# A transformer block pair in fp32 on one core: the feature-by-token products take one 512-column matmul for two of 256

## The chip, the cores and the metric

The kernel runs on one core of a Trainium2 chip. TensorE (PE) multiplies; a 128x128 tile of one operand is loaded into it (LDWEIGHTS, PEld in the profile) and the other operand moves through it, up to 512 columns at a time, into a bank of PSUM of 128 partitions by 512 fp32 numbers. VectorE (DVE), ScalarE (ACT) and GpSimd (POOL) work element by element, and SyncE (SP) issues most of the DMAs. Each engine takes its instructions in the order in which they stand in its own queue, and waits for the others by semaphores. The metric is the time of one execution in microseconds of device time, the median of the runs.

## The reference

Two blocks follow each other on 256 tokens of 1024 features, all in fp32. Cut to what matters here:

```python
def first_block(x, ...):
    h = rms_norm(x, pre_mix_norm[l])
    proj = jnp.einsum('bsd,dc->bsc', h, w_in[l])
    att_q, att_k, att_v, gdn_qkv, gdn_z, gdn_a, gdn_b = jnp.split(proj, split_points, axis=-1)
    o_att = moba_attention(att_q, att_k, att_v, rel_bias)        # 8 heads of 64
    o_gdn = gated_deltanet(gdn_qkv, gdn_z, gdn_a, gdn_b, ...)    # conv of width 4, chunks of 64
    mix = jnp.einsum('bsc,cd->bsd', jnp.concatenate([o_att, o_gdn], axis=-1), w_out[l])
    x = x + rms_norm(mix, post_mix_norm[l])
    h = rms_norm(x, pre_mlp_norm[l])
    m = einsum(square(relu(einsum(h, w_up[l]))), w_down[l])      # 1024 -> 4096 -> 1024
    return x + rms_norm(m, post_mlp_norm[l])

def second_block(x, ...):
    proj = rmsnorm(x, g_mix[l]) @ w_in[l]    # xc, gb, gc, q, k, v, g_sw, gate_a, gate_r
    y_a = (gb * conv(gc * xc)) @ w_a_out[l]
    y_r = (group_norm(retention(rotary(q), rotary(k), v)) * silu(g_sw)) @ w_r_out[l]
    x = x + (sigmoid(gate_a) * y_a + sigmoid(gate_r) * y_r) @ w_o[l]
    h2 = rmsnorm(x, g_ffn[l])
    x = x + (silu(h2 @ w_ff_gate[l]) * (h2 @ w_ff_up[l])) @ w_ff_down[l]   # width 2816
    return rmsnorm(x, g_final)
```

## The kernel before

**Products.** Every large product is made of three: an operand is split into a rounded part H (a copy to the type float32r, on ACT) and a remainder L (the operand less its rounded part, on DVE), and the product is H·H + H·L + L·H, added up in one bank. `load_w` (L208) brings 512 KB of weights by a DMA on SP's queue into one of three buffers (`raw`), and splits them into `wh` on ACT (a line shown as L144, the helper `act`) and `wl` on DVE (L147, the helper `tt`), of which there are six buffers each.

**Two shapes.** Token-by-feature products (`gemm_tok_steps`, `GemmK`, `gemm_head`) move 512 columns of weights past a loaded tile of the activations. Feature-by-token products (`gemm_ch_steps`, L271) move the 256 tokens of the activations past a loaded tile of weights: for 128 features there are eight steps over the 1024 features of the input, of three matmuls of 256 columns each (H·XH, H·XL, L·XH at L222 and L281), 24 in all. Two such rounds (f = 0, 1) fill the two halves of one bank, and `evac` reads the whole bank. These products make q, k, v of the delta rule (`qkv`, six products) and q, k of the attention (`att_in`, four), 12 products of `w_up`, the eight rotary ones (`rot_evac`), 12 of the convolution branch of block two, and 18 of `w_ff_gate` and `w_ff_up`: 60 products, 120 rounds, 960 steps of three matmuls.

**Operands.** The activations `X` are a `Chan`: tiles `xTh` and `xTl` of [128, 2, 256]. `row_T` turns a normalised row on PE and `split_T` writes both parts.

**Buffers.** `SLOTS` says how many tiles each tag of the pool in SBUF holds, `BANKS` how the eight banks of PSUM are shared: three for these products (`mm`), three for the delta rule and the transposes (`sd`), two for the attention (`at`).

**Order.** A scheduler sets each engine's order when the program is built. In the first mixer the products are steps of a generator, and `go` puts some of them between the parts of the delta rule. Its longest serial piece: the products of keys in a chunk (`m`, DVE), written to DRAM (`md`) and read back one block to a partition (`mb`), fifteen steps of substitution on POOL (`tb`, `tmpb`, `ub`), to DRAM again (`ud`) and back (`U`), which PE then needs.

Of the kernel before, what the change touches and what calls it, by code (L numbers as in the profile page):

```python
# [41 lines left out]
SLOTS = {"t": 20, "g": 26, "j": 2, "n": 4, "h": 5, "k": 8}  # L42
# [55 lines left out]
def body(ctx: ExitStack, tc: tile.TileContext, I: dict, cst: bass.AP, out: bass.AP, dbg=None):  # L98
# [70 lines left out]
    @contextmanager  # L169
    def after(what):  # L170
        """what is traced here is issued behind the last instruction of that kind"""
        if what in last:
            with tc.issue_after(last[what].ins):
                yield
        else:
            yield
# [52 lines left out]
    class Chan:  # L229
        """[feature, token] operand: pairs of 128-feature tiles, rounded part and remainder"""  # L230
# [12 lines left out]

    def gemm_tok_steps(w, c0, X, evac):
        """[token, 512 features], a step for every two rows of 128 of the weights"""
# [14 lines left out]
    def put_off(f, n):  # L260
        """f is traced n pieces of a product later"""
        later.append([n, f])
# [7 lines left out]

    def gemm_ch_steps(w, c0, X, evac):  # L271
        """[256 features, token], a step for every 128 features"""
        ps = mmps()
        for f in range(2):
            H, L = load_w(w, 0, 8, c0 + f * P, P)
            o = ps[:, f * 256:(f + 1) * 256]
            for k in range(8):
                XH, XL = X.at(k)
                mm(o, H[:, k, :], XH, k == 0, False)
                mm(o, H[:, k, :], XL, False, False)  # L280
                last["step"] = nc.tensor.matmul(o, L[:, k, :], XH, start=False, stop=k == 7)  # L281
            if f == 1:
                evac(ps)
# [13 lines left out]
    class GemmK:  # L297
        """[token, D], 128 rows of the weights at a time; at the end token tile by token tile"""
# [33 lines left out]
        def finish(self, X, tail=((0, TAIL), (1, TAIL))):  # L332
            """tail: (token tile, number of rows of 128)"""
# [12 lines left out]
    def gemm_head(groups, X):  # L346
        """two groups of [token, 512 features], six of their eight loads first for one token tile"""
# [25 lines left out]
    def split_T(ps, X, k0, t, scale=None):  # L373
        """four transposed 128-feature tiles in a bank to operands"""
# [13 lines left out]
    def rms_of(srcs, gate="xs"):  # L388
        """1 / sqrt(mean of squares + eps) over the two halves of a row"""
# [42 lines left out]
    X = Chan(8, "xT")  # L432
# [4 lines left out]
    # per-channel vectors, turned into columns  # L437
# [14 lines left out]
    # head scalars on every partition  # L452
# [12 lines left out]
    def log1p_exp_neg_abs(src, n):  # L465
        """log(1 + exp(-|src|))"""
# [11 lines left out]
    # ================= block 1: mixer =================  # L478
# [8 lines left out]
    def hb(ap):  # L487
        """[P, 8] for every one of 64 columns"""
        return ap[:, :, None].to_broadcast([P, 8, 64])

    def cb(name):
        """[P, 64] for every head"""
        return C(name)[:, None, :].to_broadcast([P, 8, 64])

    def pe(ap, e):
        """heads of parity e of a [P, 8 * 64] tile"""
        return ap.rearrange("p (a e d) -> p a e d", a=4, e=2)[:, :, e, :]

    # ---- products with w_in and attention over the one block of keys: the work that fills the
    # gaps of the delta rule; each step yields its size ----  # L500
# [5 lines left out]
    def qkv(i):  # L506
        """q, k, v of the delta rule: convolution and SiLU, [channel, token]"""
# [16 lines left out]
    def att_in(i):  # L524
        def qk_evac(ps):
            s_ = T2("aqk")
            act(s_, ps, AF.Copy)
            (QT if i < 2 else KT)[i % 2] = s_.rearrange("p (a n) -> p a n", a=2)

        yield from gemm_ch_steps(w_in, 256 * i, X, qk_evac)  # L530
# [15 lines left out]
    # relative-position bias: [q, head, key], masked where the key is ahead  # L546
# [13 lines left out]
    def bias_tile(a, e):  # L560
        """heads of parity e, pair a"""
# [6 lines left out]
    def logits(a, e):  # L568
        """heads of parity e, pairs (2a, 2a+1 of that parity)"""
# [89 lines left out]
    def go(what):  # L659
        """fill for a time, or until a mark"""  # L660
# [17 lines left out]
    # a, b  # L678
# [40 lines left out]
    # decays between the rows of a chunk, and from its start and to its end  # L719
# [30 lines left out]
    def inv_norm(p_, name):  # L750
        """1 / sqrt(sum of squares + eps) of every head's 64 columns"""
# [593 lines left out]
```

## Time and profile before

| | |
|---|---|
| three runs | 938.85, 939.85, 940.24 us; median 939.85 us |
| the profiled execution, from its first to its last instruction | 935.1 us |
| median less that span | 4.75 us |
| PE busy with matmuls | 907.8 us (97%), 6069 matmuls |
| DVE busy | 564.5 us (60%) |
| ACT busy | 455.5 us (49%) |
| POOL busy | 93.4 us (10%) |
| read from HBM | 158.59 MB, 173 GB/s over the span |

The trace has the span of the profiled execution and not what lies around it, so its own time on the scale of the runs is taken as the span and the 4.75 us that the median has beyond it. Busy times are unions: an engine that works on two instructions at once counts once. A matmul's duration in the trace is longer than the distance to the next one, since matmuls follow each other through the array; what a matmul costs in a dense stretch is the distance of its start to the next start.

### The profile page before, as it was taken

To read this page: it belongs to the slowest core of one execution; us is meant where nothing else is said; L and a number is where in the kernel's file an instruction comes from. 1 tells how busy PE (TensorE), PEld (TensorE's weight loads), DVE (VectorE), ACT (ScalarE), POOL (GpSimd) and SP (SyncE) were. 2 spreads that over 40 slices of the span, in tenths; PEclk is the share of its full clock that TensorE was granted. 3 is DMA by queue.
4 is the path that set the end of the run, shared out by engine and by line. 5 is a ranking of instruction groups with operands and counts; after the bars stand their busy time and mean duration, and the time that the engine had idled before them with its cause. 6 is when DMAs were issued, how large, how long until landed. Compare 5 with 4: busy or idle time off the path is not lost.

```text
span 935.1 us, 15099 instructions
## 1 busy us (share of the span) xinstructions
PE 907.8 (97%) x6069; PEld 805.7 (86%) x6069; DVE 564.5 (60%) x771; ACT 455.5 (49%) x641; POOL 93.4 (10%) x127
## 2 busy tenths in 40 slices
PE   5999899999999999999999999999999999999997
PEld 5798787778998888799988899988888789999886
DVE  4897445376766544877656666645456755555443
ACT  4875263356656443655455554345343545444432
POOL 4168001020000000203200000000000000000000
PEclk9999899999999999999999999999999999999999
DMA  9775532156765765576534556566474567666551
GB/s 280 195 192 147 142 119 91 46 180 183 222 182 169 241 192 176 174 225 205 183 122 151 155 170 186 176 194 199 159 225 149 168 190 204 189 182 182 184 177 45
DMA packets 177142, 162.48 MB, mean 174 GB/s; under 512 B 18941, under 2 KB 144169, under 8 KB 177073
## 3 DMA queue, kind: packets, MB, share of 16 engines
q1 hardware_dynamic: 175200, 156.49, 56.1%
q0 software_dynamic: 1728, 4.78, 1.6%
q8 instruction: 47, 0.77, 0.3%
q10 hardware_dynamic: 144, 0.26, 0.1%
q14 instruction: 23, 0.18, 0.1%
HBM read 158.59 MB, written 2.92 MB: 173 GB/s over the span
## 4 chain that ended last, share of the span: by engine, by line
PE 83%; DMA 5%; DVE 4%; ACT 3%; issue 2%; POOL 2%; SPq 0%; POOLq 0%; ACTq 0%; DVEq 0%
PE mm L222 58%; PE mm L281 10%; PE at L222 7%; PE sd L222 6%; DVE wl L147 1%; DMA raw<-in_w_in_dram 1%; DVE acc L150 1%; POOL tb L147 1%; ACT wh L144 1%; POOL tmpb L147 1%; DMA hs<-in_dec_b_dram 1%; DMA raw<-in_w_up_dram 1%; DMA U<-ud 1%; ACT junk L392 1%; DMA mb<-md 1%
## 5 line engine op out<-in xcount | busy, mean ns | idle before, releaser
L147 DVE TENSOR_TENSOR wl<-raw,wh 128x1024 fp32r<-128x1024 f32 (+1 forms) x287 | 350.1, 1225 | 261.9 <-ACT wh L144 259.2
L144 ACT ACTIVATE wh<-raw 128x1024 fp32r<-128x1024 f32 (+1 forms) x287 | 302.3, 1057 | 354.4 <-PE mm L222 133.5
L222 PE MATMUL mm<-xTh,wh 128*128 128x256 f32 x960 | 273.3, 285 | 1.0 <-ACT wh L144 1.0
L281 PE MATMUL mm<-xTh,wl 128*128 128x256 f32 x960 | 271.9, 283 | 1.8 <-DVE wl L147 1.8
L222 PE MATMUL mm<-xTl,wh 128*128 128x256 f32 x960 | 271.9, 283 | 0.0
L281 PEld LDWEIGHTS mm<-xTh,wl 128*128 128x128 f32 x960 | 184.2, 192 | 2.2 <-DVE wl L147 2.2
L222 PEld LDWEIGHTS mm<-xTh,wh 128*128 128x128 f32 x960 | 184.1, 192 | 2.1 <-ACT wh L144 1.4
L222 PEld LDWEIGHTS mm<-xTl,wh 128*128 128x128 f32 x960 | 184.2, 192 | 0.1
L222 PE MATMUL mm<-wh,xTh 128*128 128x512 f32 x264 | 104.6, 396 | 1.2 <-ACT xTh L381 1.2
L222 PE MATMUL mm<-wh,xTl 128*128 128x512 f32 x264 | 103.7, 393 | 1.5 <-DVE xTl L384 1.5
L222 PE MATMUL mm<-wl,xTh 128*128 128x512 f32 x264 | 103.6, 392 | 0.0
L222 PE MATMUL mm<-wh,hidh 128*128 128x512 f32 x162 | 63.3, 391 | 0.1
L222 PE MATMUL mm<-wl,hidh 128*128 128x512 f32 x162 | 63.3, 391 | 0.0
L222 PE MATMUL mm<-wh,hidl 128*128 128x512 f32 x162 | 63.0, 389 | 0.0
L222 PEld LDWEIGHTS mm<-wh,xTl 128*128 128x128 f32 x264 | 49.7, 188 | 13.0 <-DVE xTl L384 2.8
L222 PEld LDWEIGHTS mm<-wh,xTh 128*128 128x128 f32 x264 | 49.7, 188 | 12.8 <-ACT xTh L381 1.9
L222 PEld LDWEIGHTS mm<-wl,xTh 128*128 128x128 f32 x264 | 49.7, 188 | 10.0 <-DVE wl L147 0.2
L396 POOL TENSOR_TENSOR r<-ms,neghalf 128x1 f32<-128x1 f32 x13 | 10.7, 827 | 466.9 <-DVE ms L150 466.9
L222 PEld LDWEIGHTS mm<-wh,hidl 128*128 128x128 f32 x162 | 30.4, 188 | 6.5
L222 PEld LDWEIGHTS mm<-wh,hidh 128*128 128x128 f32 x162 | 30.5, 188 | 6.3 <-issue 0.5
L222 PEld LDWEIGHTS mm<-wl,hidh 128*128 128x128 f32 x162 | 30.5, 188 | 5.5
L392 ACT ACTIVATE junk<-x 128x512 f32<-128x512 f32 x18 | 11.3, 627 | 17.9 <-DVE x L147 12.9
(359 smaller groups left out, 1146.3 us busy)
## 6 DMA issues: line engine op xcount, KB each, us to landing
raw<-in_w_in_dram SPq DMA_DIRECT2D x116, 512.0 KB, 4.3
raw<-in_w_up_dram SPq DMA_DIRECT2D x32, 512.0 KB, 4.1
raw<-in_w_down_dram SPq DMA_DIRECT2D x32, 512.0 KB, 4.2
raw<-in_w_ff_gate_dram SPq DMA_DIRECT2D x22, 512.0 KB, 4.1
raw<-in_w_ff_up_dram SPq DMA_DIRECT2D x22, 512.0 KB, 4.5
raw<-in_w_ff_down_dram SPq DMA_DIRECT2D x22, 512.0 KB, 4.0
raw<-in_w_r_out_dram SPq DMA_DIRECT2D x16, 512.0 KB, 3.9
raw<-in_w_out_dram SPq DMA_DIRECT2D x8, 512.0 KB, 3.5
```

The lines of the kernel that those rows point to most:

```text
L144: nc.scalar.activation(o, i, f, **kw)
L147: (eng or nc.vector).tensor_tensor(o, a, b, op=op)
L150: nc.vector.scalar_tensor_tensor(o, a, s, b, op0=op0, op1=op1)
L222: nc.tensor.matmul(o, a, b, start=start, stop=stop)
L281: last["step"] = nc.tensor.matmul(o, L[:, k, :], XH, start=False, stop=k == 7)
L392: last["sq"] = nc.scalar.activation(T2("junk", tag="j"), srcs[i], AF.Square, scale=1.0 / 32, accum_out=ss[:, i:i + 1])
L396: last["pow"] = nc.gpsimd.tensor_tensor(r, ms, neghalf[:, :1], op=ALU.pow)
```

## The change

`X` becomes a `Both` in all four places: one tile [128, 2, 2, 256] for a pair of feature tiles, in which a feature tile's 256 rounded columns and its 256 remainder columns lie side by side. A step of a feature-by-token product is then two matmuls: H against both parts, 512 columns wide, which leaves H·XH in the left half of a bank and H·XL in the right half, and L·XH, 256 columns, on top of the left half. A round of 128 features so takes a bank of its own. When it is read, ACT copies the right half to SBUF and DVE adds the left half to it; two rounds make a [128, 512] tile `sum`, and `evac` reads that tile in place of the bank. For `att_in` and for `xc` in the convolution branch the `sum` tile is the result itself, and their copies of the bank are gone. The tags of the pool are shared out anew.

```diff
-SLOTS = {"t": 20, "g": 26, "j": 2, "n": 4, "h": 5, "k": 8}
+SLOTS = {"t": 12, "x4": 4, "s2": 2, "g": 24, "j": 2, "n": 4, "h": 5, "k": 8}
...
+    class Both:
+        def __init__(self, name):
+            self.b = [T2(name, F32R, [P, 2, 2, S], "x4") for _ in range(4)]
+            self.h = [b[:, :, 0, :] for b in self.b]
+            self.l = [b[:, :, 1, :] for b in self.b]
+        at = Chan.at
+        def both(self, k):
+            return self.b[k // 2][:, k % 2, :, :]
...
-    def gemm_ch_steps(w, c0, X, evac):
-        ps = mmps()
+    def gemm_ch_steps(w, c0, X, evac, into=None):
+        s_ = into or T2("sum", tag="s2")
         for f in range(2):
             H, L = load_w(w, 0, 8, c0 + f * P, P)
-            o = ps[:, f * 256:(f + 1) * 256]
+            ps = mmps()
             for k in range(8):
-                XH, XL = X.at(k)
-                mm(o, H[:, k, :], XH, k == 0, False)
-                mm(o, H[:, k, :], XL, False, False)
-                last["step"] = nc.tensor.matmul(o, L[:, k, :], XH, start=False, stop=k == 7)
+                mm(ps, H[:, k, :], X.both(k), k == 0, False)
+                last["step"] = nc.tensor.matmul(ps[:, :S], L[:, k, :], X.at(k)[0], start=False, stop=k == 7)
+            half = s_[:, f * S:(f + 1) * S]
+            act(half, ps[:, S:], AF.Copy)
+            tt(half, ps[:, :S], half, ADD)
             if f == 1:
-                evac(ps)
+                evac(s_)
...
-    X = Chan(8, "xT")
+    X = Both("xT")
...
-        gemm_ch(w2, 256 * i, X, lambda ps: act(xc, ps, AF.Copy))
+        gemm_ch(w2, 256 * i, X, lambda ps: None, xc)
```

What the change does to the order, at three places. On PE, the first product of `w_up` that is made feature by token (`mm` is the bank, `xT` the activations, `wh` and `wl` the split weights); before, two steps of its first round:

```order
L222 MATMUL mm_2479<-xTh_2163,wh_2482 128x256
L222 MATMUL mm_2479<-xTl_2167,wh_2482 128x256
L281 MATMUL mm_2479<-xTh_2163,wl_2483 128x256
L222 MATMUL mm_2479<-xTh_2164,wh_2482 128x256
L222 MATMUL mm_2479<-xTl_2168,wh_2482 128x256
L281 MATMUL mm_2479<-xTh_2164,wl_2483 128x256
```

and now the last step of its first round, four transpositions of another part (`sd`), and the first step of its second round:

```order
L222 MATMUL mm_2370<-xT_2054,wh_2366 128x512
L293 MATMUL mm_2370<-xT_2054,wl_2367 128x256
L778 MATMUL sd_2389<-ident,hf_2335 128x128 x4
L222 MATMUL mm_2404<-xT_2051,wh_2400 128x512
L293 MATMUL mm_2404<-xT_2051,wl_2401 128x256
```

Three narrow matmuls a step became a wide and a narrow one, which take turns through a round, and the second round has a bank of its own (`mm_2404`) where it had the other half of the first one's.

On DVE, one rotary product in the second block (`ra` and `rb` are the products with cosine and sine, `rot` their sum and difference, `wl` the weights of later rounds); before:

```order
L147 TENSOR_TENSOR ra_4257<-mm_4196,cs_3301 128x512
L147 TENSOR_TENSOR rb_4258<-mm_4196,cs_3301 128x512
L147 TENSOR_TENSOR wl_4446<-raw_4443,wh_4445 128x1024
L147 TENSOR_TENSOR rot_4259<-ra_4257,rb_4258 128x256
L147 TENSOR_TENSOR rot_4259<-rb_4258,ra_4257 128x256
L147 TENSOR_TENSOR wl_4488<-raw_4485,wh_4487 128x1024
```

and now:

```order
L147 TENSOR_TENSOR sum_4018<-mm_4025,sum_4018 128x256
L147 TENSOR_TENSOR wl_4233<-raw_4230,wh_4232 128x1024
L147 TENSOR_TENSOR sum_4018<-mm_4050,sum_4018 128x256
L147 TENSOR_TENSOR ra_4069<-sum_4018,cs_3065 128x512
L147 TENSOR_TENSOR rb_4070<-sum_4018,cs_3065 128x512
L147 TENSOR_TENSOR wl_4270<-raw_4267,wh_4269 128x1024
L147 TENSOR_TENSOR rot_4071<-ra_4069,rb_4070 128x256
L147 TENSOR_TENSOR rot_4071<-rb_4070,ra_4069 128x256
```

Two additions per product came in, each behind ACT's copy of the same half; the rest stands as it did.

On DVE in the first mixer, up to the last piece of `m` (`acc` is the convolution of q, k and v); before:

```order
L147 TENSOR_TENSOR wl_952<-raw_949,wh_951 128x1024
L147 TENSOR_TENSOR wl_1024<-raw_1021,wh_1023 128x1024
L147 TENSOR_TENSOR m_703<-sd_704,eb_572 128x4x64
L147 TENSOR_TENSOR m_703<-sd_705,eb_572 128x4x64
L150 SCALAR_TENSOR_TENSOR acc_692<-mm_631,chan,acc_692 128x255 x2
L150 SCALAR_TENSOR_TENSOR acc_692<-mm_631,chan,acc_692 128x254 x2
L150 SCALAR_TENSOR_TENSOR acc_692<-mm_631,chan,acc_692 128x253 x2
L147 TENSOR_TENSOR m_726<-sd_727,eb_578 128x4x64
L147 TENSOR_TENSOR m_726<-sd_728,eb_578 128x4x64
```

and now:

```order
L147 TENSOR_TENSOR sum_587<-mm_594,sum_587 128x256
L147 TENSOR_TENSOR wl_707<-raw_704,wh_706 128x1024
L147 TENSOR_TENSOR wl_805<-raw_802,wh_804 128x1024
L147 TENSOR_TENSOR m_649<-sd_650,eb_533 128x4x64
L147 TENSOR_TENSOR sum_587<-mm_619,sum_587 128x256
L150 SCALAR_TENSOR_TENSOR acc_638<-sum_587,chan,acc_638 128x255
L147 TENSOR_TENSOR m_649<-sd_651,eb_533 128x4x64
L150 SCALAR_TENSOR_TENSOR acc_638<-sum_587,chan,acc_638 128x254
```

The first ten rounds now have an addition each ahead of the last `m`, and of the remainders `wl` that stand ahead of it there are 13 where there were 15.

## Rows read from the trace of the kernel before

**Rows 1.** The page: busy time by engine; the granted TensorE clock in 40 slices.

```profile
PE 907.8 (97%) x6069; PEld 805.7 (86%) x6069; DVE 564.5 (60%) x771; ACT 455.5 (49%) x641; POOL 93.4 (10%) x127
...
PEclk9999899999999999999999999999999999999999
```

**Rows 2.** The chain that ended last, over the whole span, by engine.

```profile
PE 83%; DMA 5%; DVE 4%; ACT 3%; issue 2%; POOL 2%; SPq 0%; POOLq 0%; ACTq 0%; DVEq 0%
```

**Rows 3.** Windows: stretch, length; busy us (xinstructions) by engine, clock, DMA.

```profile
22.00:63.00 41.00, 37.32 (x319) 33.31 (x320) 35.41 (x70) 32.74 (x50) 15.26 (x11) 1.00 0.71 195
...
408.00:451.00 43.00, 43.00 (x359) 42.91 (x358) 33.99 (x47) 20.96 (x24) 12.48 (x7) 1.00 0.69 204
539.00:605.00 66.00, 66.00 (x552) 66.00 (x551) 44.15 (x61) 28.74 (x34) 1.06 (x2) 1.00 0.59 176
762.00:866.00 104.00, 104.00 (x864) 103.63 (x864) 58.51 (x60) 49.61 (x59) 0.00 (x0) 1.00 0.66 191
```

**Rows 4.** Groups by line: two of the three matmuls of a step.

```profile
L222 PE MATMUL mm<-xTh,wh 128*128 128x256 f32 x960 | 273.3, 285 | 1.0 <-ACT wh L144 1.0
...
L222 PE MATMUL mm<-xTl,wh 128*128 128x256 f32 x960 | 271.9, 283 | 0.0
```

**Rows 5.** Timeline of PE in a rotary product: first and seventh of seven starts.

```profile
429.76 0.28 PE L222 MATMUL mm<-xTl,wh 128*128 128x256 f32 x1
...
430.48 0.28 PE L222 MATMUL mm<-xTl,wh 128*128 128x256 f32 x1
```

**Rows 6.** Chain in `w_down`, where all matmuls are 512 columns wide (start, length).

```profile
324.96 2.04 PE mm L222 x9
327.68 2.04 PE mm L222 x9
```

**Rows 7.** Timeline of PE in a step of `w_ff_down`, which has both widths.

```profile
880.92 0.28 PE L222 MATMUL at<-wh,hidh 128*128 128x256 f32 x1
881.03 0.28 PE L222 MATMUL at<-wl,hidh 128*128 128x256 f32 x1
881.15 0.28 PE L222 MATMUL at<-wh,hidl 128*128 128x256 f32 x1
...
881.63 0.40 PE L222 MATMUL mm<-wh,hidh 128*128 128x512 f32 x1
881.87 0.40 PE L222 MATMUL mm<-wl,hidh 128*128 128x512 f32 x1
```

**Rows 8.** Chain in the same product: two steps, nine wide matmuls of each.

```profile
881.80 2.07 PE mm L222 x9
...
884.58 2.07 PE mm L222 x9
```

**Rows 9.** Groups by line on DVE and ACT: shapes, mean ns of one.

```profile
L147 DVE TENSOR_TENSOR wl<-raw,wh 128x1024 fp32r<-128x1024 f32 (+1 forms) x287 | 350.1, 1225 | 261.9 <-ACT wh L144 259.2 <-PE mm L222 2.2
L144 ACT ACTIVATE wh<-raw 128x1024 fp32r<-128x1024 f32 (+1 forms) x287 | 302.3, 1057 | 354.4 <-PE mm L222 133.5 <-PE at L222 52.9 <-issue 45.5
...
L384 DVE TENSOR_TENSOR xTl<-sd,xTh 128x256 fp32r<-128x256 f32 x16 | 6.0, 416 | 0.2 <-ACT xTh L381 0.2
...
L147 DVE TENSOR_TENSOR ra<-mm,cs 128x512 f32<-128x512 f32 x8 | 5.5, 688 | 2.6 <-PE mm L281 2.5
...
L381 ACT ACTIVATE xTh<-sd 128x256 fp32r<-128x256 f32 x16 | 5.2, 380 | 4.2 <-PE sd L419 4.2
...
L147 DVE TENSOR_TENSOR rot<-ra,rb 128x256 f32<-128x256 f32 x8 | 3.3, 417 | 0.0
```

**Rows 10.** Chain between `m` and `U` (start, length).

```profile
63.05 2.56 DMA md<-m
...
90.72 5.09 DMA U<-ud
```

**Rows 11.** Timeline of PE where `U` arrives.

```profile
95.95 0.44 PE L222 MATMUL sd<-U,b 64*64 64x64 f32 x2 [4.33 <-DMA U<-ud]
```

More of the change, by code (lines that the diff above doesn't have):

```diff
@@ L524, in att_in, with qk_evac @@
     def att_in(i):
-        def qk_evac(ps):
-            s_ = T2("aqk")
-            act(s_, ps, AF.Copy)
+        s_ = T2("aqk")
+        def qk_evac(_):
             (QT if i < 2 else KT)[i % 2] = s_.rearrange("p (a n) -> p a n", a=2)
-        yield from gemm_ch_steps(w_in, 256 * i, X, qk_evac)
+        yield from gemm_ch_steps(w_in, 256 * i, X, qk_evac, s_)
     def z_in():
@@ L1036, in body @@
     wb1, wb2 = row_bcast("post_mix_norm"), row_bcast("pre_mlp_norm")
-    X = Chan(8, "xT")
+    X = Both("xT")
     for t in range(2):
@@ L1083, in body @@
     wb1, wb2 = row_bcast("post_mlp_norm"), row_bcast("g_mix_2")
-    X = Chan(8, "xT")
+    X = Both("xT")
     for t in range(2):
@@ L1244, in body @@
     wb1, wb2 = row_bcast("g_ffn_2"), row_bcast("g_final_2")
-    X = Chan(8, "xT")
+    X = Both("xT")
     for t in range(2):
```

## The prediction

> **What bounds the kernel now.** I read the busy times first, then the chain that ended last, then windows over the stages with these products, and only then single matmuls. TensorE is busy 97% of the span at the full granted clock but for one slice of 40 [rows 1], and 83% of the chain that ended last is its work [rows 2]. In the rotary, convolution and FFN stages its busy time is the whole window, while DVE is busy 34.0 of 43 us, 44.2 of 66 and 58.5 of 104, and ACT less [rows 3]. There the time is the sum of the matmuls' distances and nothing else. It is different in the first mixer before `U` arrives: between 22 and 63 us PE is busy 37.3 of 41 us, DVE 35.4, ACT 32.7 [rows 3], and the chain goes from engine to engine until `m` goes out at 63.05; from there to the arrival of `U` at 95.81 (90.72 and 5.09) it is DMAs and the substitution on POOL [rows 10], and PE stands idle for the last 4.33 us of it [rows 11]. A matmul saved before that point buys only a longer wait.
>
> **What a step costs, before and after.** The 960 steps are the groups of 960 [rows 4]. Their durations (283 to 285 ns) overlap, so I take distances of starts. Seven narrow matmuls start from 429.76 to 430.48: 0.72 us in six distances, 0.120 us each [rows 5]. Nine wide ones take 2.04 us, 0.2267 each [rows 6]. At 2.4 GHz, the full clock, 256 columns are 0.1067 us and 512 are 0.2133, so both widths carry the same 0.0133 us on top. A step of three narrow ones is 0.360 us; a wide and a narrow one are 0.2267 + 0.120 = 0.3467, and 0.0133 less. The columns that move are as many as before; what goes is one matmul with its weight load.
>
> The trace before nowhere has wide and narrow in turn. The nearest rows are the steps of `w_ff_down`, with nine wide and six narrow ones. The first narrow one after a wide one is followed after 0.11 us (880.92 to 881.03), the first wide one after a narrow one after 0.24 (881.63 to 881.87) [rows 7]. Their sum is 0.35, which agrees with 0.3467. The bounds: 0.2267 + 0.11 = 0.34 if the short distance holds every time and the long one never, and 0.24 + 0.12 = 0.36 if it is the other way round. I take 0.3467, since it is what the rates give and what the two distances next to a change of width add up to. So a step gives back 13.3 ns, at the bounds 20 and nothing.
>
> On this fixed part the Trainium skill says otherwise: "TensorE: Matmul & The Clock Gate", section "Back-to-back issue gap", has a warm distance of N/2.4 ns and 2.5 ns more. By that a step would give back 2.5 ns, and the 816 steps below 2 us in place of 10.9. The trace has 13.3 ns at both widths, and the measurement decides; no row shows why it is larger.
>
> **Where it counts.** After `U`: 12 products of `w_up`, 8 rotary, 12 of the convolution branch, 18 of the FFN are 50 products of 16 steps, 800; one product of `att_in` (16 steps) is also left behind `U`, so 816. 816 x 13.3 ns = 10.9 us less (16.3 and 0 at the bounds). The other 144 steps stand ahead of `U` and are counted at nothing; the chain through POOL covers them.
>
> **What is added.** Each of the 120 rounds gets a copy of 128x256 from a bank on ACT, like `xTh`, 0.380 us, and an addition of 128x256 from a bank on DVE, like `xTl`, 0.416 [rows 9].
> - In the dense stages they cost nothing as long as PE stays the slowest. The tightest is the rotary stage: DVE has per product 2 x 1.225 (`wl`), 2 x 0.688 (`ra`, `rb`), 2 x 0.417 (`rot`), 4.66, and with 2 x 0.416 5.49 us [rows 9], against 16 x 0.3467 = 5.55 on PE. That is 99%, but by durations, which overlap where instructions follow closely. ACT has 2 x 1.057 + 2 x 0.380 and a copy of half a `wh`'s size: under 4. If DVE came out 0.1 us over 5.55, eight products would cost 0.8 us. In the FFN two products give DVE 4 x 0.416 more on some 6.5 of 11.1 us (58.5/104 of 11.5) [rows 3].
> - ACT's copy waits for the end of its round, and behind it in ACT's queue stands a later round's `wh`, for which `wl` on DVE waits. Six buffers of each mean that these weights are wanted five rounds (5 x 2.77 us) later; without that cover each round would wait for 0.38 + 1.06 + 1.23 us. A bank is now filled every round, and wanted again three rounds on: the copy and the addition have two rounds, 5.5 us, for 0.8 us of work and at most one `wh` and one `wl` ahead of it.
> - The fewer slots of tag `t` make the last two of the 14 remainders of the `w_up` result wait until `w_down` has read the first tiles. They are wanted 24 steps of 2.72 us into it, as the tables for the decays are wanted after it. Nothing.
> - At the ends of these stages the reader of the last bank changes from two instructions of 512 columns to two of 256. I count nothing.
> - In the first mixer DVE gets ten additions ahead of the last `m`, 4.2 us, and two `wl` less, 2.45 us: 1.7 us net. Nothing is the lower bound, since part of the convolution now starts after the first round; 4.2 the upper. I take 1.7, for DVE is 86% busy there [rows 3] and most of it should show. It delays `m`, hence `U` and all behind it. On SP's queue 21 weight loads stand ahead of the DMAs that wait for the substitution, where 24 did; the rounds ahead of `U` need 19, so PE finds its weights.
>
> **Sum.** 935.1 - 10.9 + 1.7 = 925.9 us of span; with the 4.75 us that the median has beyond it **930.7 us**, 1.0% less than 939.85. A change of 0.2% (1.9 us) is about what a measurement of this kernel can tell from none.
>
> **Rivals.**
> - **The change of width is itself paid for.** A step of `w_ff_down` takes 2.78 us (881.80 to 884.58) [rows 8], where 9 x 0.2267 + 6 x 0.120 make 2.76: going over to narrow and back costs 0.020 us. Were that due in every step, it would be 0.3667 against 0.360, 816 x 6.7 ns = 5.4 us more, with the mixer 7.1: 947 us, slower. It decides from a cost of 13.3 ns a turn on. For it: the nine wide ones take 2.07 us there, not 2.04. Against it: the excess lies also in later wide ones (2.07 - 9 x 0.2267 is 0.03, the first distance has only 0.013 of it), which here never come.
> - **The fixed part does not go with the matmul.** If the pair costs 0.36, the bound above, PE gains nothing, and the time is 939.85 + 1.7 = 941.6: no change, just. The page's 2.5 ns would put it near there as well.
> - **Dearer in the mixer.** If the two new instructions stand one behind the other in the chain to `m` in all ten rounds, that is 10 x 0.796 = 8.0 us, and the time 939.85 - 10.9 + 8.0 = 937. For it: the chain there already passes over ACT and DVE. Against it: two of them work on different rounds.
> - **More than counted.** If the narrow one is always 0.11, the step is 0.34: 939.85 - 16.3 + 1.7 = 925.
>
> **How the numbers follow.** The forecast with its term for the mixer between 0 and 4.2 has 0.58, the gain of 16 us 0.12, the dear mixer 0.06: faster. The pair at 0.36 has 0.11, no change. The paid change of width has 0.13, slower. Small mixtures of them take 0.04 from the faster ones to no change. So faster 0.72, the same 0.15, slower 0.13. The range goes from 923.5 (16.3 us gained, nothing lost) to 941.6 (nothing gained on PE, 1.7 lost) and leaves out the slower case. The forecast's own range is 929 to 933.2.
>
> **What would show it.** Starts of a wide and the next wide matmul 0.347 us apart in the rotary, convolution and FFN stages, 2.77 us a round; PE busy in all of these windows; DVE near 95% in the rotary stage, with no wait of PE for `wl`; `md` out at about 65 us and `U` about 1.7 us later than 95.8, the idle time of PE before it about 1 us longer. I would be wrong if steps take over 0.353 us, if PE waits for banks or weights in a dense stage, or if `m` comes over 4 us later.

## The result and the profile after

The change takes 946.86 us (median of four runs, 945.52 to 948.23) against 940.05 for the kernel before: 1.0067 times, with a 95% interval of 1.005 to 1.0085. It is slower, by 0.7%, where 930.7 us was forecast, and lies outside the range of 923.5 to 941.6. Its profiled execution has a span of 946.5 us and a time of 948.23.

The page of the changed kernel, busy times, the granted clock in 40 slices and the chain that ended last:

```profile
PE 907.4 (96%) x5109; PEld 757.5 (80%) x5109; DVE 611.6 (65%) x891; ACT 485.3 (51%) x753; POOL 93.6 (10%) x127
...
PEclk9899799999999999999999999999999999999999
...
PE 75%; DMA 8%; DVE 6%; issue 4%; ACT 3%; POOL 2%; SPq 0%; POOLq 0%; ACTq 0%; DVEq 0%
```

960 matmuls went, and PE's share of the chain fell from 83% [rows 2] to 75%: DMAs, VectorE and waits took their places. Windows of the first mixer, the rotary stage, the convolution branch and the FFN (columns as in [rows 3]):

```profile
22.00:68.00 46.00, 41.86 (x255) 33.22 (x254) 38.97 (x76) 34.51 (x57) 15.27 (x11) 0.89 0.55 152
418.00:470.00 52.00, 49.55 (x269) 41.35 (x269) 47.60 (x67) 30.17 (x45) 13.07 (x7) 1.00 0.69 199
556.00:617.00 61.00, 61.00 (x354) 53.36 (x353) 47.70 (x79) 31.26 (x49) 1.06 (x2) 1.00 0.65 186
787.00:878.00 91.00, 91.00 (x517) 78.95 (x516) 62.09 (x84) 53.15 (x85) 0.00 (x0) 1.00 0.65 193
```

PE fills the last two, as before. In the rotary stage it no longer does, and DVE is at 92% (47.60 of 52). In the first mixer the granted clock is 0.89, where it was 1.00 [rows 3].

Lengths of stages in us tell where the time went. They are read from PE's timeline of each trace, between the same matmuls: the first with the state of the delta rule (`sd<-st,wt`), the first of `w_down`, the first of keys and queries in block two (`sd<-roth,roth`), the first of `w_a_out`, the first of `w_ff_down`, and the last; 6.4 us follow behind it in each of them. `e5` is the kernel before once more and `e15` the change once more (below).

| trace (span) | to the state | to `w_down`: `w_up` | to keys x queries: rotary | to `w_a_out`: convolution | to `w_ff_down`: FFN | rest |
|---|---|---|---|---|---|---|
| before (935.1) | 146.9 | 144.9 | 169.7 | 187.6 | 218.7 | 61.0 |
| e5, before (937.1) | 148.8 | 145.0 | 169.6 | 187.6 | 218.8 | 61.0 |
| the change (946.5) | 158.9 | 144.7 | 173.2 | 185.1 | 217.1 | 61.1 |
| e15, the change (941.9) | 156.0 | 143.4 | 173.4 | 185.1 | 216.6 | 61.1 |
| e1, old form in the first mixer | 149.7 | 147.4 | 172.1 | 185.1 | 216.8 | 61.1 |
| e3, U ahead of loads | 150.7 | 144.5 | 172.2 | 185.1 | 216.7 | 61.1 |
| e6, five banks | 161.1 | 141.6 | 168.8 | 185.1 | 216.9 | 60.9 |
| e12, all mends, grouped | 146.4 | 141.9 | 168.6 | 185.6 | 215.5 | 61.0 |

Two traces of one kernel differ by 2 us (before) and 4.6 us (the change), mostly in the first mixer, where DMAs are waited for; the convolution branch agrees to 0.1 us. By these traces the change loses 7 to 12 us in the first mixer and some 3.6 in the stage with the rotary products, and gains 2.5 in the convolution branch, about 2 in the FFN and 0.2 to 1.6 around `w_up`.

**The first mixer.** SyncE's timeline around `U` in the changed kernel:

```profile
94.02 0.37 SPq L880 DMA_DIRECT2D td<-tb  x1
94.69 0.67 SPq L881 DMA_DIRECT2D ud<-ub  x1
95.45 7.59 SPq L210 DMA_DIRECT2D raw<-in_w_in_dram  x4
103.09 1.63 SPq L579 DMA_DIRECT2D bias<-vd  x1
104.85 1.28 SPq L928 DMA_DIRECT2D U<-ud  x2
```

Four weight loads now stand between the write of `ud` and the reads of `U`, where two stood before. Three of them go out at once; the fourth, at 102.67, waits until VectorE is done with the buffer `raw` of the first. The reads go out 10.2 us behind the write, where before they went out 4.0 behind it, as soon as it had landed (in that trace the reads start at 90.72 [rows 10], and the write at 86.68):

```profile
86.68 0.62 SPq L866 DMA_DIRECT2D ud<-ub  x1
```

The loads were held up in turn: they stood behind `td`, which waits for the substitution. What that did to PE, in the chain:

```profile
94.06 0.61 POOL ub L879
...
95.45 4.80 DMA raw<-in_w_in_dram
...
100.33 0.07 ACT wh L144
...
101.30 0.59 ACT qt L144
```

The first load arrives at 100.25, its `wh` stands ahead of `qt` in ACT's queue, and PE, idle for 8.2 us, waits for `qt`. It does not wait for `U` here: it comes to `U` at 111.55, without a wait, behind the work that `qt` had held up.

```profile
101.93 3.07 PE L222 MATMUL sd<-qt,kt 64*64 64x64 f32 x48 [8.16 <-ACT qt L144]
...
111.55 0.33 PE L222 MATMUL sd<-U,b 64*64 64x64 f32 x2
```

Ahead of that, `md` goes out at 69.16, 6.1 us later than before [rows 10], and its write takes 4.42 us to land for 2.56. VectorE's timeline there, and GpSimd's beside it:

```profile
61.44 0.59 DVE L150 SCALAR_TENSOR_TENSOR acc<-sum,chan,acc 128x255 f32<-128x255 f32 x1
61.96 0.41 DVE L147 TENSOR_TENSOR m<-sd,eb 128x256 f32<-128x256 f32 x1
62.29 4.71 DVE L150 SCALAR_TENSOR_TENSOR acc<-sum,chan,acc 128x254 f32<-128x254 f32 x4
66.93 0.41 DVE L147 TENSOR_TENSOR m<-sd,eb 128x256 f32<-128x256 f32 x1
...
63.14 1.22 POOL L147 TENSOR_TENSOR kbe<-kn,fb 128x512 f32<-128x512 f32 x1
64.32 1.22 POOL L147 TENSOR_TENSOR kd<-kn,er 128x512 f32<-128x512 f32 x1
```

Four `acc` take 4.71 us, 1.18 apart; the last six ahead of `m` took 2.41 us before, 0.39 apart, reading the bank:

```profile
59.33 2.41 DVE L150 SCALAR_TENSOR_TENSOR acc<-mm,chan,acc 128x255 f32<-128x255 f32 x6
```

They now read `sum`, so that both operands lie in SBUF.

The waits cost more than their length, since the clock fell with them. Windows from the start to the state, before and after, and the same 48 matmuls as above in the trace of e3:

```profile
0.00:146.90 146.90, 129.88 (x1308) 114.00 (x1308) 91.32 (x165) 83.17 (x144) 50.79 (x78) 0.98 0.64 175
...
0.00:158.90 158.90, 134.47 (x1147) 109.75 (x1147) 99.03 (x185) 87.18 (x160) 50.63 (x78) 0.92 0.58 161
...
87.99 1.86 PE L223 MATMUL sd<-qt,kt 64*64 64x64 f32 x48
```

PE is idle for 24.4 us of this stage, where it was idle for 17.0, and busy for longer with fewer matmuls. In the change the granted clock is 0.50 (1.2 GHz for 2.4) in four stretches, from 28.55, 62.68, 79.75 and 96.82 us on, each in or behind a wait of PE, of 1.7, 0.9, 2.8 and 8.2 us. PE works in them for 18.0 us (14.9 in e15), where before it had one such stretch, behind its wait for `U`, with 5.5 us of work (10.2 us in two stretches of e5). The 48 matmuls take 3.07 us at this clock and 1.86 at the full one. So some 2 to 6 us of the 7 to 12 are the clock, by an estimate: the 4.7 to 12.5 us that PE works more at half the clock, of which it loses 0.39, as these 48 do, to one half.

**Dense stages.** PE's timeline in the convolution branch (first and seventh wide start, six pairs apart) and in the FFN:

```profile
599.92 0.40 PE L222 MATMUL mm<-xT,wh 128*128 128x512 f32 x1
...
602.00 0.40 PE L222 MATMUL mm<-xT,wh 128*128 128x512 f32 x1
...
810.04 0.40 PE L222 MATMUL mm<-xT,wh 128*128 128x512 f32 x1
...
812.16 0.40 PE L222 MATMUL mm<-xT,wh 128*128 128x512 f32 x1
```

A pair takes 2.08/6 = 0.3467 us in the one, as forecast, and 2.12/6 = 0.3533 in the other. Over all pairs of a stage, by their starts, it is 353.3 ns in `w_up`, 352.3 in the rotary stage, 346.7 in the convolution branch and 352.8 in the FFN. And PE waits where these stages begin, for banks (`sum`) and once for an operand (`vl`):

```profile
243.71 0.50 PE L222 MATMUL mm<-xT,wh 128*128 128x512 f32 x1 [0.75 <-DVE sum L147]
420.57 0.50 PE L222 MATMUL mm<-xT,wh 128*128 128x512 f32 x1 [0.84 <-DVE vl L147]
433.64 0.50 PE L222 MATMUL mm<-xT,wh 128*128 128x512 f32 x1 [0.68 <-DVE sum L147]
```

VectorE's timeline at the first of them:

```profile
242.09 1.23 DVE L147 TENSOR_TENSOR wl<-raw,wh 128x1024 fp32r<-128x1024 f32 x1 [1.38 <-ACT wh L144]
243.24 0.42 DVE L147 TENSOR_TENSOR sum<-mm,sum 128x256 f32<-128x256 f32 x1
```

ACT's copy for that `sum` had ended at 242.34, but VectorE stood at a `wl` for weights that had only just arrived; PE got the bank only behind both.

### The profile page after: what moved, and what is told of

The parts are those of the page before. It is cut to its first block, busy times and chain, and to the rows that moved or that the text cites. A ratio compares the mean times of both kernels' runs of the same rounds, so it can differ in the third digit from the quotient of the medians.

```text
span 946.5 us, 13372 instructions
## 1 busy us (share of the span) xinstructions
PE 907.4 (96%) x5109; PEld 757.5 (80%) x5109; DVE 611.6 (65%) x891; ACT 485.3 (51%) x753; POOL 93.6 (10%) x127
## 4 chain that ended last, share of the span: by engine, by line
PE 75%; DMA 8%; DVE 6%; issue 4%; ACT 3%; POOL 2%; SPq 0%; POOLq 0%; ACTq 0%; DVEq 0%
PE mm L222 52%; PE mm L293 9%; PE sd L222 7%; PE at L222 6%; DMA raw<-in_w_in_dram 4%; DVE wl L147 2%; ACT wh L144 2%; DMA raw<-in_w_up_dram 2%; POOL tmpb L147 1%; DVE sum L147 1%; ACT junk L407 1%; DMA raw<-in_w_ff_up_dram 1%; DMA wb<-in_pre_mix_norm_dram 1%; DVE rot L147 1%; DVE acc L150 1%
## 5 line engine op out<-in xcount | busy, mean ns | idle before, releaser
L222 PE MATMUL mm<-xT,wh 128*128 128x512 f32 x960 | 346.5, 404 | 3.6 <-DVE sum L147 1.4
L293 PE MATMUL mm<-xT,wl 128*128 128x256 f32 x960 | 272.1, 283 | 4.5 <-DVE wl L147 4.4
L222 PEld LDWEIGHTS mm<-xT,wh 128*128 128x128 f32 x960 | 183.1, 191 | 50.1 <-DVE sum L147 2.8
L293 PEld LDWEIGHTS mm<-xT,wl 128*128 128x128 f32 x960 | 184.1, 192 | 5.6 <-DVE wl L147 5.4
L222 PE MATMUL mm<-wh,xT 128*128 128x512 f32 x528 | 168.3, 393 | 3.4 <-DVE xT L399 1.5
L222 PEld LDWEIGHTS mm<-wh,xT 128*128 128x128 f32 x528 | 98.7, 188 | 26.1 <-DVE xT L399 2.8
L222 PE MATMUL mm<-wl,xT 128*128 128x512 f32 x264 | 103.7, 393 | 0.0
L222 PEld LDWEIGHTS mm<-wl,xT 128*128 128x128 f32 x264 | 49.6, 188 | 10.7 <-DVE wl L147 0.7
L411 POOL TENSOR_TENSOR r<-ms,neghalf 128x1 f32<-128x1 f32 x13 | 10.7, 825 | 435.4 <-DVE ms L150 435.4
L147 DVE TENSOR_TENSOR sum<-mm,sum 128x256 f32<-128x256 f32 x104 | 43.5, 418 | 12.4 <-ACT sum L144 12.4
L144 ACT ACTIVATE sum<-mm 128x256 f32<-128x256 f32 x104 | 38.2, 367 | 1.9 <-PE mm L293 1.9
```

What stands on the lines that cost most here:

```text
L144: nc.scalar.activation(o, i, f, **kw)
L147: (eng or nc.vector).tensor_tensor(o, a, b, op=op)
L222: nc.tensor.matmul(o, a, b, start=start, stop=stop)
L293: last["step"] = nc.tensor.matmul(ps[:, :S], L[:, k, :], X.at(k)[0], start=False, stop=k == 7)
L411: last["pow"] = nc.gpsimd.tensor_tensor(r, ms, neghalf[:, :1], op=ALU.pow)
```

## The experiments

Theory A: the loss is made in the first mixer. B, the rival: the dense stages lose. C: VectorE is held up by GpSimd when it reads two operands from SBUF. D: `U` is late for its place in SyncE's queue. E: at the entries of the dense stages PE waits for banks. F: the price of a pair depends on a rhythm, a pattern of distances between starts that repeats. Ratios are to the kernel before on the same chip, with 95% intervals. The medians of before lay between 938.6 and 940.8 us on the chips used, so that a difference of two medians from different chips is uncertain by some 2 us.

**e1, the old form in the first mixer.** `qkv` and `att_in` call the old loop, which reads the bank.

```diff
...
-        yield from gemm_ch_steps(w_in, 1536 + 256 * i, X, conv_evac)
+        yield from gemm_ch_steps(w_in, 1536 + 256 * i, X, conv_evac, None, False)
...
```

> Products ahead of the second norm in the first mixer (q, k, v of the delta rule and q, k of the attention) in the old form of three narrow matmuls, read from the bank; all later products as in the change. Theory A, the loss is made in the first mixer (the trace of the change is 12.1 us late there and 11.3 at the end): the last m is written out at about 63 us as before, U arrives at about 96, and the median comes to 935 to 939 us. Theory B, the dense stages lose (pairs of unlike width, sums to make): nothing comes back, 945 to 948.

939.14 us, 0.9983 (0.997 to 0.9996). The first stage is back at 149.7 us, and the time is 7.7 us below the change and 1.7 below before: A holds for most of the loss, and B falls as its main cause. But it is the worst end of what was expected, for `w_up` and the rotary stage still lose 2.4 and 2.5 us to e5; in `w_up` PE waits 1.9 us for a bank, and then the clock is at 0.50 for 3.4 us.

**e2, the sum written back into the bank.** `first` is the bank of round 0; for `att_in` and `xc` ACT copies it to SBUF.

```diff
...
-            tt(half, ps[:, :S], half, ADD)
+            tt(first[:, f * S:(f + 1) * S], ps[:, :S], half, ADD)
             if f == 1:
-                evac(s_)
...
+                evac(first)
```

> The change, but VectorE writes the sum back into the bank of the first round, and every reader reads a bank as in the kernel before. Theory C, VectorE is held up where it reads two operands from SBUF while GpSimd works: the last six acc instructions of the first mixer, 0.59 to 1.26 us in the change, are 0.48 again, ra in the rotary products 0.69 instead of 1.33; m goes out 3 to 4 us earlier and the median falls by 3 to 6 us, to 941 to 944. Rival, these instructions were long for their place in the order: they stay long, and the time stays at 946 to 948.

957.99 us, 1.0183 (1.0157 to 1.0209), a miss: 11 us slower than the change. The durations are as theory C has them, and `md` goes out at 62.96, 6.2 us earlier than in the change. VectorE and GpSimd in the rotary stage, of the change first and then of this kernel:

```profile
440.67 1.33 DVE L147 TENSOR_TENSOR ra<-sum,cs 128x512 f32<-128x512 f32 x1
441.93 0.68 DVE L147 TENSOR_TENSOR rb<-sum,cs 128x512 f32<-128x512 f32 x1
...
439.58 1.88 POOL L147 TENSOR_TENSOR rotl<-rot,roth 128x512 fp32r<-128x512 f32 x1 [3.70 <-PE mm L293]
```

```profile
445.76 0.69 DVE L147 TENSOR_TENSOR ra<-mm,cs 128x512 f32<-128x512 f32 x1
...
444.73 1.82 POOL L147 TENSOR_TENSOR rotl<-rot,roth 128x512 fp32r<-128x512 f32 x1 [4.10 <-ACT roth L144]
```

`ra` beside `rotl` takes 1.33 us from SBUF and 0.69 from the bank; `rb`, which comes when `rotl` is over, 0.68 in both. The time went to banks, of which there are three and one is now held for two rounds. PE's waits for them in this kernel, beside one of 7.83 us in the first mixer; behind the second the clock is at 0.50 for some 6 us more:

```profile
244.62 0.50 PE L222 MATMUL mm<-xT,wh 128*128 128x512 f32 x1 [3.20 <-DVE mm L147]
...
431.84 0.80 PE L222 MATMUL mm<-xT,wh 128*128 128x512 f32 x1 [3.15 <-DVE mm L147]
```

**e3, `U` ahead of four loads.**

```diff
+        with after("U" if 21 <= len(started) < 26 else None):
-        nc.sync.dma_start(raw, ...)
+            nc.sync.dma_start(raw, ...)
...
```

> The change, but the four weight loads that stand between the write of ud and the reads of U in SyncE's queue are issued behind these reads. Theory D, U is late because its reads are queued behind loads that wait for buffers: they go out some 4 us after ub is done instead of 10.2, and the median falls by 4 to 6 us, to 941 to 943. Rival, the weights are what is late: PE waits for weights in place of U, and the time stays at 946 to 948.

939.90 us, 0.9987 (0.9974 to 1.0001), 7.0 less than the change, a little more than expected. SyncE's timeline:

```profile
90.89 0.76 SPq L882 DMA_DIRECT2D ud<-ub  x1
94.98 1.29 SPq L929 DMA_DIRECT2D U<-ud  x2
```

4.1 us, as before, and `qt` has no `wh` of these loads ahead of it: PE then waits 1.21 us for `U`. So the place of the loads in SyncE's queue is the largest single price, but e3 doesn't show theory D as it was put. It moves both what stood ahead of `U` and what stood ahead of `qt`, and in the change PE waited for `qt`. Nor is the price waiting alone: up to the state PE idles for 21.2 us instead of 24.4, and works at the lower clock for 6.8 us instead of 18.0.

**e4, the kernel before with a copy of the bank**, for the delta rule and the rotary products.

```diff
+                    s_ = T2("sum")
+                    act(s_, ps, AF.Copy)
+                    ps = s_
                 evac(ps)
...
```

> The kernel before with its three narrow matmuls, but for q, k, v of the delta rule and for the rotary products ScalarE copies the whole bank to SBUF (some 0.6 us each), and the convolution and the rotation read the copy. Theory C (VectorE held up by GpSimd when it reads two operands from SBUF): ra goes from 0.69 to 1.3 us in the rotary stage where GpSimd works, the last six acc of the first mixer from 0.40 (spacing) to about 1.2, m goes out 3 to 4 us later, and the median rises by 2 to 5 us, to 942 to 945. Rival, the long instructions belong to the new products: durations stay at 0.69 and the time at 940.

949.92 us, 1.0095 (1.0075 to 1.0114). The last six `acc` of the first mixer:

```profile
58.72 7.37 DVE L150 SCALAR_TENSOR_TENSOR acc<-sum,chan,acc 128x255 f32<-128x255 f32 x6 [1.66 <-ACT acc L144]
```

7.37 us for 2.41, with no pair in the kernel: the long instructions don't belong to the new products. `ra` was a miss: it stayed at 0.68 us, for its copy came when `rotl` was over, and the stage kept its length (169.7). The rise of 9.1 us, all in the first stage (160.2 us), is more than the 5 us of these six; the rest was not told apart. PE works at the lower clock for 10.6 us of it.

**e5, the kernel before again.**

> The kernel before, unchanged, for a second trace. The times of before in these runs are spread from 938.1 to 943.3 us, so its spans from 936 to 941, and the execution whose trace the prediction used had 935.1. If that execution was a quick one, this trace is 2 to 5 us longer, and it shows where; the dense stages should agree to 0.1 us, and the difference lie in the first mixer, where DMAs are waited for. Rival: the difference is spread over all stages.

Span 937.1 us: 1.9 more in the first mixer, all else within 0.1. The execution behind the prediction was a quick one; the 4.75 us taken as lying beyond its span are 2.1 in the runs that list both.

**e6, five banks behind the first mixer.**

```diff
-            ps = mmps()
+            ps = atps() if dense and f else mmps()
```

> The change, but behind the first mixer the second round of each product takes a bank of the attention, so that five banks take turns where three did. Theory E, at the entry of w_up and of the rotary stage PE waits for banks, since the sums stand in VectorE's queue behind wl, which waits for late weights: these waits of PE (0.75, 1.1 and 0.96 us are the longest) go, and the median falls by 2 to 5 us, to 942 to 945. Rival, the weights themselves are late: PE waits as long for wh or wl instead, and the time stays at 946 to 948.

941.36 us, 1.0017 (1.0 to 1.0034), 5.5 less than the change, a little more than expected. No wait of PE for a bank is left in `w_up` and the rotary stage, and these become 3.4 and 0.8 us shorter than in e5. Not all of it is banks: `w_up` fell into the quick rhythm here, 346.9 ns a pair, which is worth 1.2 us (192 x 6.4 ns). `ra` still takes 1.33 us beside GpSimd, and the rotary stage is no longer than before: with banks to spare that costs nothing.

**e7 and e8, what was found put together.** Old form in the first mixer, five banks, and the rotary products in the old form (e7), or as pairs summed in a bank (e8, whose line is shown).

```diff
...
-        gemm_ch(w2, 3072 + 256 * i, X, rot_evac)
+        gemm_ch(w2, 3072 + 256 * i, X, rot_evac, None, "bank")
...
```

> As e1_old_mixer, with the five banks of e6_dense_banks, and the eight rotary products in the old form of three narrow matmuls too, read from the bank. By theories A, C and E together: from 939.1 us the entry of w_up gives back 2 to 4.5, the rotary stage 2.7, so 932 to 934.5 us. If the pairs bring nothing in w_up, the convolution branch and the FFN: 938 to 941.

> As e7_old_mixer_rot, but the rotary products are pairs again and their sum is written back into the bank of the first round, from which ra and rb are read. By theory C ra stays at 0.69 us beside GpSimd and the rotary stage now gains 1.7 us over before, where it lost 2.7 in e1_old_mixer: 930 to 933 us. Rival, banks held for two rounds or VectorE at 5.5 us per product stop PE: 934 to 939.

934.19 us, 0.993 (0.9905 to 0.9956), and 933.10, 0.9923 (0.9903 to 0.9942). e7 came as expected, e8 at the edge: its rotary stage gains 0.4 us over e5 and not 1.7, in part since a pair takes 353.2 ns there (128 x 6.8 ns are 0.9 us). The 1.1 us between the two are within the noise.

**e9 and e10, the whole change, mended.** e9 is pairs everywhere with e3, e6 and the rotary sum of e8; e10 sums q, k, v of the delta rule in banks too, by the line shown.

```diff
...
-        yield from gemm_ch_steps(w_in, 1536 + 256 * i, X, conv_evac)
+        yield from gemm_ch_steps(w_in, 1536 + 256 * i, X, conv_evac, None, True, True)
...
```

> The whole change, pairs in the first mixer too, with e3_U_ahead and e6_dense_banks together, and the rotary sum in the bank as in e8. If the two waits (U's reads behind loads, PE behind banks) are separate, their prices add: 946.9 - 7 - 5.5, so 933 to 936 us. Rival, both took from the same slack: 937 to 940.

> As e9_all_pairs_mended, but in the first mixer q, k, v of the delta rule too are summed into the bank of the first round and read from there, with two banks of the attention, which wait for nothing yet, as the second ones. Theory C: the six acc beside GpSimd take 0.48 us and not 1.2, m goes out 3 to 4 us earlier than in e9, and the median is 2 to 4 us lower. Rival, m waits for something else or PE for banks held longer, as in e2: no gain, or a loss.

936.92 us, 0.9971 (0.9958 to 0.9985), and 943.65, 1.0039 (1.0025 to 1.0053). e9 ends just above what was expected. The prices of e3 and e6 nearly add up in it (9.9 of 12.5 us), though it has the rotary sum of e8 besides. Where they come back its one trace doesn't show: it is of the slowest of twelve executions (940.71 us), and its first stage takes 157.6 us. e10 is a miss: its `acc` take 0.47 us, but the chain shows what came instead:

```profile
71.09 1.65 POOL rnq L147
72.94 1.14 DVE wl L147
...
74.12 0.39 SPq L211
...
74.69 4.38 DMA mb<-md
```

The read of `md` now stands behind a load in SyncE's queue, which waits for a `wl`, which stands behind a wait for GpSimd: a load in the way once more, at another place. It goes out 6.9 us behind `md`, where before that took 2.6.

**e11, e12 and e14, a round by groups:** the eight wide matmuls first, then the eight narrow ones, in e8, in e10 and in the change itself.

```diff
             for k in range(8):
                 mm(ps, H[:, k, :], X.both(k), k == 0, False)
+            for k in range(8):
                 last["step"] = nc.tensor.matmul(ps[:, :S], L[:, k, :], X.at(k)[0], start=False, stop=k == 7)
```

> As e8_old_mixer_rotbank, but within a round the eight wide matmuls come first and then the eight narrow ones. Theory F: in turn a pair falls into one of two rhythms, 346.6 ns in the convolution branch and 353.4 in w_up, the rotary stage and the FFN; by groups it is 8 x 226.7 + 8 x 120 ns a round and some 20 ns for the change of width everywhere. Then 60 rounds of w_up and the FFN get 34 ns shorter each (2.0 us), 16 rotary ones 0.5, the convolution's 24 get 20 ns longer (0.5): 930.5 to 932 us. Rival, the 353.4 belong to these operands or banks in any order: 933 or more.

> As e10_conv_from_bank, in the order of e11_grouped. What e11 gains over e8 comes here too: 1 to 2.5 us below e10. Rival, the remainders wl, wanted later in a round, hold their buffers longer and late weights get later in the first mixer: no gain over e10.

> The change with the eight wide matmuls of a round first and the eight narrow ones behind them, nothing else. Theory F alone (the rhythm of the pairs): e11 gained 2.2 us over e8 by it, so 944 to 945.5. Rival, the order gives the remainders wl and so ACT, VectorE and the loads more time, most of all in the first mixer (e12 was 15.4 us below e10): 930 to 940.

930.86 us, 0.9905 (0.9888 to 0.9921), 2.2 less than e8, which ran on another chip; 928.22, 0.9876 (0.9858 to 0.9895), 15.4 less than e10; 944.11, 1.006 (1.0046 to 1.0075), 1.6 less than e15. PE's timeline of e11:

```profile
799.89 2.00 PE L222 MATMUL at<-xT,wh 128*128 128x512 f32 x8
801.73 1.12 PE L309 MATMUL at<-xT,wl 128*128 128x256 f32 x8
802.68 0.63 PE L222 MATMUL mm<-xT,wh 128*128 128x512 f32 x2
```

A round is 2.79 us, 0.349 a pair, in every stage. By theory F that is dearer than in turn in the convolution branch (+0.5 us in the table) and cheaper than the slow rhythm elsewhere. What the order alone is worth the medians of e14 and e15 don't show, since their intervals overlap; the pairs, at 353 and 346.7 ns in turn, make it some 1.5 us, an estimate. e12 is a miss, by its size: what it gains over e10 is nearly all in the first mixer (146.4 us against 162.0). There `mb` is read 3.5 us behind `md` and not 6.9, PE idles for 17.9 us instead of 29.4, and it works at the lower clock for 3.4 us instead of 12.2. Why the order does this there and not in e14 (157.1 us) was not tried. e12, the whole change with these mends, is the fastest here, faster than both kernels.

**e13, GpSimd's `kbe` and `kd` put behind the substitution.**

```diff
+        with after("sub"):
-        tt(h8(kbe), h8(kn[t]), hb(tile_h(FB, t)), MUL, nc.gpsimd)
+            tt(h8(kbe), h8(kn[t]), hb(tile_h(FB, t)), MUL, nc.gpsimd)
...
```

> The change, but GpSimd makes kbe and kd (four products of SBUF operands, 1.2 us each, wanted only behind U) behind the substitution, so that it does nothing while VectorE makes the last acc and m; the order of VectorE is the same. Theory C: the last six acc, 0.59 to 1.26 us in the change, take 0.48 (0.40 apart), the last m comes 3.5 us and not 7.8 behind the first, m goes out about 4 us earlier, and the median falls by 3 to 4.5 us, to 942.5 to 944. Rival, m goes out earlier, but U is late for its place behind the loads in SyncE's queue: 945 to 947.

945.24 us, 1.0072 (1.0049 to 1.0096); the change beside it 945.71. VectorE's timeline:

```profile
60.77 0.59 DVE L150 SCALAR_TENSOR_TENSOR acc<-sum,chan,acc 128x255 f32<-128x255 f32 x1
61.28 0.41 DVE L147 TENSOR_TENSOR m<-sd,eb 128x256 f32<-128x256 f32 x1
61.62 2.36 DVE L150 SCALAR_TENSOR_TENSOR acc<-sum,chan,acc 128x254 f32<-128x254 f32 x4
63.90 0.41 DVE L147 TENSOR_TENSOR m<-sd,eb 128x256 f32<-128x256 f32 x1
```

With its order unchanged, the four `acc` take 2.36 us for 4.71 (the first of them still 1.18, beside the last work of GpSimd). `md` goes out 2.8 us earlier, counted from the first matmul of `kt`. That nothing of it can be seen in the median fits the rival, since `U` is read 9.5 us behind `ud` here too, and PE again waits 8.31 us for `qt`; but the first mixers of two traces differ by as much, and 2 us can't be told from none by these runs. So theory C is shown for the durations and for `m`; what it adds to the time is not.

**e15, the change again.**

> The change once more, to compare these runs on one chip and for a second trace: 945.5 to 948.2 us as measured, so a median of 946 to 948. The dense stages should agree with the first trace to 0.1 us, waits at their entries included, if they come from the order and not from chance.

945.71 us, 1.0069 (1.0052 to 1.0087), just under what was expected. The stages of its trace behind `w_down` agree with the first within 0.5 us (0.1 was expected), those ahead of it not; what moved there was not looked into.

## Why the prediction failed

The sum had 1.7 us more for the first mixer, where the traces have 7 to 12, and 10.9 less for the pairs, where they have 6.9; waits at the entries of the dense stages and the clock stood in it at nothing. Two signs of being wrong that the prediction named came clearly: PE waits for banks in a dense stage, and `m` comes 6.1 us later; the third, steps over 0.353 us, only just.

- **What failed first is the sentence on SyncE's queue** in the step on the first mixer: that 21 loads instead of 24 ahead of the DMAs of the substitution still give PE its weights. The weights of the rounds were not the point. The three loads that no longer came ahead came behind, between `ud` and `U`, and the `wh` of the first of them holds `qt` up in ACT's queue, for which PE waits 8.2 us; the prediction had PE wait for `U`, about 1 us longer than 4.33. What was to be counted is what a load is queued behind and what is queued behind it. Price: 7.0 us by e3, a part of it through the clock.
- **"DVE gets ten additions, 1.7 us net" had the wrong items.** The additions are there, but the readers changed their price: the last `acc` went from 0.39 to 1.2 us apart, 2.8 us of `m` by e13, of which its median shows nothing. The prediction took the readers of `sum` at the durations of readers of the bank, though GpSimd was at work beside them in the trace of before (`kbe` and `kd`). This is a rule of the Trainium skill ("SBUF — State Buffer", section "Who interferes with whom"): a VectorE instruction with two inputs in SBUF contends with a GpSimd instruction that reads SBUF, one with at most one, outside its two-port modes, does not. The traces agree (1.33 against 0.69 us), and the prediction should have weighed it.
- **The clock was taken as full.** "TensorE is busy 97% of the span at the full granted clock but for one slice of 40" is right for the trace before, but the sum prices a longer wait at its length alone. In the change the waits of the first mixer took PE to 0.50 of the clock for 18.0 us of its work (14.9 in e15), where it had 5.5 (10.2 in e5): some 2 to 6 us by the estimate above. No run holds the clock and changes the rest, so that this share is not shown by an experiment.
- **"In the dense stages they cost nothing as long as PE stays the slowest"** holds within the stages and fails at their entries. The cover that was named, three banks and "at most one `wh` and one `wl` ahead", was right in size for weights that are there; at an entry the `wl` itself waits for weights, with the `sum` behind it. Price: 5.5 us by e6, of which 1.2 are the quick rhythm.
- **The price of a pair was mis-sized.** 13.3 ns a step is what the convolution branch gave: 192 x 13.3 = 2.6 us, 2.5 in the table. The others gave 360 less 353.3, 352.3 and 352.8: 192 x 6.7 + 128 x 7.7 + 288 x 7.2 = 4.3 us where 608 x 13.3 = 8.1 stood. So 6.9 us of 10.7. In e13 the FFN fell into the quick rhythm, and its stage was 215.2 us, 3.6 less than in e5, where 3.8 was forecast: the term is sound where the rhythm is quick. The 2.5 ns on top of N/2.4 in the Trainium skill's "Back-to-back issue gap" ("TensorE: Matmul & The Clock Gate") are given there for an isolated matmul, which the prediction passed over; the rows of before have 13.3. (816 x 2.5 ns are 2.04 us and not below 2.)
- **The rivals.** The one that ended at 947 us came near the time by another mechanism: the change of width costs 0 to 7 ns a pair and not 20. "Dearer in the mixer" was the right place; it named two instructions a round, not queues and GpSimd.
- **The conversion** of span to median was 2.6 us too high (4.75 taken, 2.1 measured), as the shown execution was a quick one; the forecast is the median less 9.2 either way.

By the stages of the table the first mixer takes 7 to 12 us more and the rotary products some 3.6, `w_up` takes 0.2 to 1.6 less and the two others 2.5 and about 2. The spans differ by 4.8 to 11.4 us, according to which traces are taken, and the medians by 6.8.

## What to carry to other kernels

When a change moves weight loads in a queue, look at the transfers of the serial chain in the same queue, at what each load waits for and at the instructions behind its first reader: the place of a few loads cost about as much here, 7.0 us by e3, as the pairs gained, 6.9. Ask too what a longer wait does to the granted clock behind it. When results move from PSUM to SBUF, price their readers anew, with what GpSimd does beside them. And a stage that is bound by one engine in its middle can be bound by buffers at its entry; two more banks were worth some 4 us there.

## What the runs showed of the hardware

A wide and a narrow matmul in turn settle into one of two rhythms, and stay in it for tens of pairs or for a whole stage: starts 112, 233, 117, 231 ns apart (346.5 a pair) or 117, 241, 120, 236, 113, 233 (353.3). Within a stage it can go over from one to the other: `w_up` of e3 starts with 353 and goes on with 347. Operands don't decide it: `w_up` has 346.9 in e6 and 352.5 in e8, with the same loop and banks; the FFN had the quick one throughout (346.7) in e13 alone, the convolution branch in every run in turn but e2, where PE waits. What decides it stays open. By groups of eight the pair costs 349 ns everywhere.

`tensor_tensor` on 128x512 with both operands in SBUF took VectorE 1.33 us beside a GpSimd instruction of 1.88 us, and 0.68 when that was over or 0.69 with one operand in a bank. Behind waits of PE the granted clock was at 0.50 for stretches of 3.4 to 10.2 us; 48 matmuls of 64x64 took 3.07 us there and 1.86 at 1.00.
